# Softmax attention's keys normalised and rotated in the linear attention's last slots and passed on through DRAM

## The chip, the cores and the metric

The kernel runs on one core of a Trainium2 chip. The core has a matrix engine (TensorE, PE in the profile; its weight loads are a row of their own, PEld), a vector engine (VectorE, DVE), a scalar engine (ScalarE, ACT), a general engine (GpSimd, POOL, unused here) and a sync engine (SyncE, SP) whose queue issues nearly all DMA transfers. The engines run side by side, each through its own queue in order, and wait for each other on semaphores. SBUF is the on-chip memory of 128 partitions, PSUM the accumulators that PE writes, DRAM the memory outside. The metric is the time of one execution on the device in microseconds (us); lower is better.

## The reference

One encoder block over 1024 tokens of width 1024: two branches read the same normalised input, their gated sum goes through an output projection, and a feed-forward part follows. Cut to what matters here:

```python
h = _rms_norm(x, norm_mix_g[l])
proj = h @ w_in[l]          # q,k,v,r and gate codes of the linear attention; q,k,v of the softmax attention; gates
y_gla = _gla_branch(...) @ w_o_gla[l]
y_swa = _swa_branch(s_q, s_k, s_v, ...) @ w_o_swa[l]
merged = jax.nn.sigmoid(gate_a) * y_gla + jax.nn.sigmoid(gate_b) * y_swa
x = x + merged @ w_out[l]
x = x + (silu(gate) * up) @ w_ffn_out[l]      # with rms norm and w_ffn_in before
```

In the softmax attention branch the keys (2 heads of 128) and queries (8 heads of 128) are normalised per token and head, multiplied by a gain, and rotated; then each block of 128 tokens attends to itself and its two neighbours:

```python
q = _rope(_rms_norm(q.reshape(bsz, s, SWA_HEADS, hd), q_g), pos)
k = _rope(_rms_norm(k.reshape(bsz, s, hkv, hd), k_g), pos)
# _rope: concatenate([x1 * cos - x2 * sin, x2 * cos + x1 * sin])
```

The change moves the second of these two lines.

## The kernel before, in words

All products keep float32 accuracy: an operand is split into a high part (ACT copies it, rounded) and a low part (DVE subtracts), and three matmuls are added (`mm3`, L78). Weights stream from DRAM through `wunit` (L66): a load on SP, the high part on ACT, the low part on DVE.

The program runs through these stages, in order of time: input, statistics and the first projections (to about 250 us); the linear attention (to about 522 us); the softmax attention (to about 748 us); the gates and the output projection; the feed-forward part. The five remaining token-wise projections and eight feature-wise ones are not a stage of their own. They are generators of single matmuls in the list `dense` (L669), and both attentions are cut into slots: `slot` (L206) calls the parts of a slot and puts a given number of these matmuls between them (`fill`, L193), so that PE has work while the other engines prepare the next part. `need` (L202) runs `dense` on until a result has been stored.

PE's order is the order of the code, since both loops stand in `tc.manual_schedule` for that engine. The order of ACT, DVE and SP is made by a scheduler at build time: an earlier line goes first among what is ready, and what is not ready lets later lines pass. Once built, each queue runs in that order. Memory comes from pools of named tiles; a tag with `bufs=2` has two buffers, and a third tile of that tag waits for the first. A pool opened on the memory of closed pools waits until these are free as a whole.

- The first stage's pools are closed at L470 (`g0s.close()`). The linear attention's constants go into the pool `gc` (L472): `lrS` and `upS` (the gate codes and the gate weights, split), `mask`, and `tri`, loaded at L479. `upr` (L483) and `lrf` (L493) are the loads from which `upS` (L484, L485) and `lrS` (L495 to L498) are made.
- The linear attention's working tiles are in `gt` (L502, helper `gtile`, L509). It has 4 heads of 8 chunks, 46 slots (0 to 45). `at[t, j]` names the part `j` of slot `t`: `g_gates` (0), `g_powers` (6), `g_scores` (1), `g_out` (2), `g_back_out` (3), `g_turn` (4 or 5). The order within a slot is the tuple at L689. From slot 36 on only `g_back_out` and `g_turn` are left, and a slot has 12 dense matmuls, 18 in the last two. `g_turn` stores the output with `o<-ot` (L667).
- `proj_t("skv", 2)` is the third generator of `dense`. For each block `t` of 128 tokens it stores 512 values a token, two keys and two values, into the DRAM tile `scr["skv", t]` (L187).
- `glas.close()` (L690) frees the linear attention's pools. The softmax attention's constants are loaded from L707 on: `cosb`, `sinb`, `band`, `qg`, `kg`, `sink`.
- Its slots (`todo`, L894 on) hold, for key block `t`: `k_load` (L762) loads the block of keys and values into one tile `kvr` with one buffer; `k_prep` (L772) splits the values (`vSh`, `vSl`) and calls `norm_rope` (L735) for the keys; `k_turn` (L779) transposes the keys on PE into `kTh` and `kTl`. For queries: `a_load`, `a_prep`, `a_turn`, `a_scores` (maxima on DVE at L823, exponentials on ACT at L838), `a_probs` (transposed probabilities, copied at L858 and L859), `a_out`.
- `rsqrt` (L95) is Ln and Exp on ACT and four small DVE instructions that refine the result.

Of the kernel before, what the change touches and what calls it, by code (L numbers as in the profile page):

```python
# [8 lines left out]
F32 = mybir.dt.float32  # L9
FR = mybir.dt.float32r  # L10
U32 = mybir.dt.uint32
AF = mybir.ActivationFunctionType
ALU = mybir.AluOpType

P = 128
T = 1024
KT = 8
HT = 512
NH = 4
NC = 8  # L20
EPS = 1e-6
# [9 lines left out]
def body(tc, i, out):  # L31
    nc = tc.nc
    with ExitStack() as root:
# [8 lines left out]
        def nm(s):  # L42
            uid[0] += 1
            return f"{s}_{uid[0]}"
# [4 lines left out]
        def chtile(shape, dt=F32):  # L49
            return psc.tile(list(shape), dt, tag="ch", name=nm("ch"))  # L50
# [4 lines left out]
        def scratch(name, shape=(P, 512)):  # L55
            return dram.tile(list(shape), F32, tag=name, name=name)
# [4 lines left out]
        def load_const(pool, name, src, shape, dt=F32):  # L61
            t = pool.tile(list(shape), dt, tag=name, name=name)
            nc.sync.dma_start(out=t, in_=src)
            return t
# [23 lines left out]
        epst = cst.tile([P, 1], F32, tag="eps", name="eps")  # L88
# [6 lines left out]
        def rsqrt(dst, v, scale, epsv, eps_t, pool, shape, tag, tags=None):  # L95
            tags = tags or (tag + "l", tag + "t")
            l = pool.tile(list(shape), F32, tag=tags[0], name=nm("rl"))
            nc.scalar.activation(l, v, AF.Ln, bias=eps_t[:, 0:1], scale=scale)
            nc.scalar.activation(l, l, AF.Exp, scale=-0.5)
            t = pool.tile(list(shape), F32, tag=tags[1], name=nm("rt"))  # L100
            nc.vector.tensor_scalar(t, v, scale, epsv, op0=ALU.mult, op1=ALU.add)
            nc.vector.tensor_tensor(t, t, l, op=ALU.mult)
            nc.vector.scalar_tensor_tensor(t, t, -0.5, l, op0=ALU.mult, op1=ALU.mult)
            nc.vector.scalar_tensor_tensor(dst, t, 1.5, l, op0=ALU.add, op1=ALU.mult)
# [10 lines left out]
        scr = {}  # L115
# [77 lines left out]
        def fill(n):  # L193

            while n > 0 and dense:
                try:
                    next(dense[0])
                    n -= 1
                except StopIteration:
                    dense.pop(0)  # L200

        def need(key):  # L202
            while key not in scr:
                fill(12)

        def slot(stages, n):  # L206

            stages = [f for f in stages if f] or [lambda: None]
            done = 0
            for j, f in enumerate(stages):  # L210
                f()
                t = n * (j + 1) // len(stages)
                fill(t - done)
                done = t
# [195 lines left out]
        with tc.manual_schedule(engines={mybir.EngineType.PE}):  # L410
# [8 lines left out]
            for k in range(KT):  # L419
# [5 lines left out]
                c = slice((k % 4) * P, (k % 4 + 1) * P)  # L425
# [17 lines left out]
            for f in range(0, NG, 2):  # L443
                x_first(f)
                if f == 0:
                    for s in range(2):
                        v = chtile((P, HT))
# [22 lines left out]
        g0s.close()  # L470

        gc = glas.enter_context(tc.tile_pool(name="gc", bufs=1))  # L472
        lrS = gc.tile([98, T], FR, tag="lrS", name="lrS")
        upS = gc.tile([98, 2, 512], FR, tag="upS", name="upS")

# [13 lines left out]
        for s in range(2):  # L489
            c = slice(s * HT, (s + 1) * HT)  # L490
# [11 lines left out]
        gt = glas.enter_context(tc.tile_pool(name="gt", bufs=2))  # L502
# [6 lines left out]
        def gtile(tag, shape=(P, 256), dt=F32, bufs=2):  # L509
            return gt.tile(list(shape), dt, tag=tag, name=nm(tag), bufs=bufs)  # L510
# [148 lines left out]
        def g_turn(hd, c):  # L659
# [6 lines left out]
            for j in range(2):  # L666
# [2 lines left out]
        dense += [proj_t("v0", 0), proj_t("v1", 1), proj_t("skv", 2), proj_t("sq0", 3),  # L669
                  proj_t("sq1", 4)] + [proj_f(f"r{m}", 8 + m) for m in range(8)]  # L670

        at = {}
        last = 0
        for n in range(NH * NC):
            hd, c = divmod(n, NC)
            cb = hd * NC + NC + 4 + (NC - 1 - c)
            tt = cb + c % 2 + 2
            for j, (t, f) in enumerate(((n, g_gates), (n + 2, g_scores), (n + 4, g_out),
                                        (cb, g_back_out), (tt, g_turn))):
                if j or c % 2 == 0:  # L680
                    at[t, j + (j == 4 and c % 2)] = (f, hd, c)
                last = max(last, t)
            if c % 2 == 0:
                at[n + 1, 6] = (g_powers, hd, c)
        with tc.manual_schedule(engines={mybir.EngineType.PE}):
            fill(24)
            for t in range(last + 1):
                n = 46 if t < 2 else 30 if t < 4 else 15 if t < NH * NC + 4 else 12 if t < last - 1 else 18
                slot([(lambda v=at[t, j]: v[0](*v[1:])) if (t, j) in at else None for j in (0, 6, 5, 4, 3, 2, 1)], n)  # L689
        glas.close()  # L690


# [3 lines left out]
        sc_ = swas.enter_context(tc.tile_pool(name="swc", bufs=1))  # L696
        swe = swas.enter_context(tc.tile_pool(name="swe", bufs=2))
        stg = stgs.enter_context(tc.tile_pool(name="stg", bufs=4, side="right"))
        swl = stgs.enter_context(tc.tile_pool(name="swl", bufs=2, side="right"))
        swm = stgs.enter_context(tc.tile_pool(name="swm", bufs=1, side="right"))  # L700

        class sw:
            def tile(shape, dt, tag, name, bufs=2):
                pool = swm if tag in ("p", "ph", "pl") else swe if tag in (
                    "kvr", "sq2", "qn2", "sq4", "qn4", "qr", "qh", "ql") else swl
                return pool.tile(shape, dt, tag=tag, name=name, bufs=bufs)
        cosb = load_const(sc_, "cosb", i["c_cos"], (P, KT, 64))  # L707
        sinb = load_const(sc_, "sinb", i["c_sin"], (P, KT, 64))
        band = load_const(sc_, "band", i["c_band"], (P, 384))
        qg = load_const(sc_, "qg", i["qg"], (P, P))  # L710
        kg = load_const(sc_, "kg", i["kg"], (P, P))
        sink = load_const(sc_, "sink", i["sink"], (P, 8))
        kTh = sc_.tile([P, 2, T], FR, tag="kTh", name="kTh")
        kTl = sc_.tile([P, 2, T], FR, tag="kTl", name="kTl")
# [12 lines left out]
        def inv_norm(raw, n, sq, scale, epsv, eps_t):  # L727
            ss = sw.tile([P, n], F32, tag=f"ss{n}", name=nm("ss"))
            nc.scalar.activation(sq, raw[:, 0:n], AF.Square)
            nc.vector.tensor_reduce(ss, sq, axis=mybir.AxisListType.X, op=ALU.add)  # L730
            rs = sw.tile([P, n], F32, tag=f"rs{n}", name=nm("rs"), bufs=4)
            rsqrt(rs, ss, scale, epsv, eps_t, sw, (P, n), f"sn{n}")
            return rs

        def norm_rope(raw, n, t, gain, scale, epsv, eps_t):  # L735

            sq = sw.tile([P, n, P], F32, tag=f"sq{n}", name=nm("sq"))
            rs = inv_norm(raw, n, sq, scale, epsv, eps_t)
            qn = sw.tile([P, n, P], F32, tag=f"qn{n}", name=nm("qn"))
            for h in range(n):  # L740
                nc.vector.scalar_tensor_tensor(qn[:, h], raw[:, h], rs[:, h:h + 1], gain,
                                               op0=ALU.mult, op1=ALU.mult)
            c = cosb[:, t:t + 1].to_broadcast([P, n, 64])
            s = sinb[:, t:t + 1].to_broadcast([P, n, 64])
            b = sq
            nc.vector.tensor_tensor(b[:, :, 0:64], qn[:, :, 64:128], s, op=ALU.mult)
            nc.vector.tensor_tensor(b[:, :, 64:128], qn[:, :, 0:64], s, op=ALU.mult)
            nc.vector.tensor_tensor(qn[:, :, 0:64], qn[:, :, 0:64], c, op=ALU.mult)
            nc.vector.tensor_tensor(qn[:, :, 64:128], qn[:, :, 64:128], c, op=ALU.mult)
            nc.vector.tensor_tensor(qn[:, :, 0:64], qn[:, :, 0:64], b[:, :, 0:64], op=ALU.subtract)  # L750
            nc.vector.tensor_tensor(qn[:, :, 64:128], qn[:, :, 64:128], b[:, :, 64:128], op=ALU.add)
            return qn

        for h in range(8):
            for s in range(2):
                scr["b", h, s] = scratch(f"b{h}_{s}")
# [1 line left out]
        keys, att = {}, {}  # L758

        raws = {}  # L760

        def k_load(t):  # L762
            raws[t] = sw.tile([P, 4, P], F32, tag="kvr", name=nm("kvr"), bufs=1)
            need(("skv", t))
            nc.sync.dma_start(out=raws[t].rearrange("p a b -> p (a b)"), in_=scr["skv", t])

        def a_load(g, n):
            need((f"sq{g}", n))
# [1 line left out]
            nc.sync.dma_start(out=raws[g, n].rearrange("p a b -> p (a b)"), in_=scr[f"sq{g}", n])  # L770

        def k_prep(t):  # L772
            kv = raws.pop(t)
            v2 = kv[:, 2:4].rearrange("p a b -> p (a b)")
            nc.scalar.activation(vSh[t], v2, AF.Copy)
            nc.vector.tensor_tensor(vSl[t], v2, vSh[t].bitcast(F32), op=ALU.subtract)
            keys[t] = norm_rope(kv[:, 0:2], 2, t, kg, 1.0 / 128, EPS, epst)

        def k_turn(t):  # L779
            kt = chtile((P, 2, P))  # L780
# [114 lines left out]
        for n in range(2 * KT):  # L895
            g, t = divmod(n, KT)
# [5 lines left out]
            if n < KT:  # L902
                todo[n + 1].append((k_turn, n))
                todo[n].append((k_prep, n))
                if n:
                    todo[n - 1].append((k_load, n))
            todo[n].append((a_load, g, t))
        order = (a_probs, k_prep, a_prep, a_scores, a_turn, k_turn, a_out, k_load, a_load)
        k_load(0)
        with tc.manual_schedule(engines={mybir.EngineType.PE}):  # L910
            for t, v in enumerate(todo):
# [507 lines left out]
```

## Time and profile before

| what | value |
|---|---|
| median of 3 runs | 1643.52 us (1643.13 to 1643.59) |
| the profiled execution's own time | 1642.39 us, with a span of 1640.6 us |
| mean granted PE clock | 1.000 |
| DMA | 252.38 MB, mean 154 GB/s |
| raw keys and values stored (`skv<-st`) | 8, issued from 408.2 to 456.9 us |
| `kvr<-skv` loads in the attention | 8, issued from 526.6 to 593.9 us, 3.2 us to landing in the middle |
| DVE busy at 580 to 600, 600 to 620 us | 19.50 and 19.46 of 20 us |
| ACT busy at 330 to 400 us | 62.82 of 70 us |

How to read it: the span is from the first to the last instruction of the program. A row of the timeline gives start, duration, engine, line, operation, the tile written and the tiles read, shapes, a count where equal rows are merged, and in brackets how long the engine had been idle and what ended that. The matmuls overlap each other, so a duration of 0.39 us stands beside a start every 0.23 us. A row of waits reads "who waited <- for whom: us in total, times, longest". Starts count from the start of the span. "SPq" rows are DMA issues on SP's queue.

### The profile page before, as it was taken

How to read it: one execution, taken by the hardware profiler on the slowest of the kernel's cores; microseconds unless marked ns; L12 is line 12 of the kernel's file. 1: busy time of each engine (PE TensorE's matmuls, PEld its weight loads, DVE VectorE, ACT ScalarE, POOL GpSimd, SP SyncE). 2: the span in 40 equal slices, each digit the busy share in tenths (PEclk: the TensorE clock that was granted, in tenths of full speed). 3: DMA queues.
4: the chain of work that ended last, by engine and by line, in shares of the span. 5: the costliest groups of instructions: out<-in, count | busy, mean ns of one | idle time of the engine just before them, and what ended most of it. 6: DMA issues, size and time to landing. Idle time of an engine off the chain costs nothing.

```text
span 1640.6 us, 23222 instructions
## 1 busy us (share of the span) xinstructions
PE 1632.3 (99%) x7636; PEld 1357.1 (83%) x7636; DVE 1239.0 (76%) x2548; ACT 878.3 (54%) x1847; POOL 0.2 (0%) x4
## 2 busy tenths in 40 slices
PE   9999999999999999999999999999999999999999
PEld 7888888888888888887888888888888888888887
DVE  8766666788854998757885678877777788789655
ACT  8522234789986788775554557333333333354442
POOL 0000000000000000000000000000000000000000
PEclk9999999999999999999999999999999999999999
DMA  7444336444436533248765554443334443596433
GB/s 237 142 140 148 113 100 191 145 125 144 148 116 187 180 97 109 83 130 261 243 211 179 166 150 140 146 143 116 103 119 144 142 147 129 181 338 194 149 98 119
DMA packets 157497, 252.38 MB, mean 154 GB/s; under 512 B 18142, under 2 KB 43486, under 8 KB 157376
## 3 DMA queue, kind: packets, MB, share of 16 engines
q1 hardware_dynamic: 157376, 250.90, 48.5%
q8 instruction: 60, 0.98, 0.3%
q14 instruction: 61, 0.50, 0.1%
HBM read 183.46 MB, written 67.37 MB: 153 GB/s over the span
## 4 chain that ended last, share of the span: by engine, by line
PE 94%; DVE 2%; DMA 2%; ACT 1%; issue 0%; SPq 0%; ACTq 0%; DVEq 0%
PE mm L76 32%; PE mm L306 9%; PE mm L308 9%; PE mm L307 9%; PE ch L76 8%; PE mm L1232 7%; PE ch L1232 5%; PE ch L306 4%; PE ch L308 4%; PE ch L307 4%; PE ch L855 1%; DMA kvr<-skv 1%; DMA lo<-b 0%; PE ch L663 0%; PE ch L584 0%; PE ch L805 0%
## 5 line engine op out<-in xcount | busy, mean ns | idle before, releaser
L298 ACT ACTIVATE wh<-ws 128x512 fp32r<-128x512 f32 x132 | 83.3, 632 | 198.0 <-PE mm L307 103.9
L70 ACT ACTIVATE wh<-wr 128x512 fp32r<-128x512 f32 x226 | 140.7, 628 | 83.6 <-PE mm L76 59.7
L72 DVE TENSOR_TENSOR wl<-wr,wh 128x512 fp32r<-128x512 f32 x226 | 154.4, 687 | 36.5 <-ACT wh L70 35.9
L76 PE MATMUL mm<-wh,xh 128*128 128x512 f32 x320 | 132.3, 413 | 0.2 <-ACT st L186 0.2
L76 PE MATMUL mm<-wh,xl 128*128 128x512 f32 x320 | 130.6, 408 | 0.0
L76 PE MATMUL mm<-wl,xh 128*128 128x512 f32 x320 | 130.5, 408 | 0.0
L299 DVE TENSOR_TENSOR wl<-ws,wh 128x512 fp32r<-128x512 f32 x132 | 90.7, 687 | 29.6 <-ACT wh L298 28.4
L298 ACT ACTIVATE wh<-wr 128x512 fp32r<-128x512 f32 x69 | 43.6, 632 | 123.7 <-issue 49.6
L298 ACT ACTIVATE wh<-a 128x512 fp32r<-128x512 f32 x64 | 40.5, 633 | 90.3 <-PE ch L1232 42.3
L299 DVE TENSOR_TENSOR wl<-a,wh 128x512 fp32r<-128x512 f32 x64 | 44.2, 691 | 42.2 <-ACT wh L298 40.6
L76 PEld LDWEIGHTS mm<-wh,xh 128*128 128x128 f32 x320 | 60.4, 189 | 10.7 <-ACT st L186 0.6
L76 PEld LDWEIGHTS mm<-wl,xh 128*128 128x128 f32 x320 | 60.3, 189 | 10.3
L1232 PE MATMUL mm<-hh,wh 128*128 128x512 f32 x176 | 68.6, 390 | 0.0
L1232 PE MATMUL mm<-hh,wl 128*128 128x512 f32 x176 | 68.6, 389 | 0.0
L1232 PE MATMUL mm<-hl,wh 128*128 128x512 f32 x176 | 68.5, 389 | 0.0
L76 PEld LDWEIGHTS mm<-wh,xl 128*128 128x128 f32 x320 | 60.4, 189 | 9.8
L76 PE MATMUL mm<-xh,wh 128*128 128x512 f32 x160 | 65.6, 410 | 0.0
L76 PE MATMUL mm<-xl,wh 128*128 128x512 f32 x160 | 63.8, 399 | 0.0
L76 PE MATMUL mm<-xh,wl 128*128 128x512 f32 x160 | 56.5, 405 | 0.0
L1202 DVE TENSOR_TENSOR hl<-hr,hh 128x512 fp32r<-128x512 f32 x75 | 51.5, 686 | 4.5 <-ACT hh L1201 4.5
L1232 PE MATMUL ch<-hh,wl 128*128 128x512 f32 x132 | 51.4, 390 | 0.0
L1232 PE MATMUL ch<-hh,wh 128*128 128x512 f32 x132 | 51.4, 389 | 0.0
(566 smaller groups left out, 4877.3 us busy)
## 6 DMA issues: line engine op xcount, KB each, us to landing
wr<-in_w_fi_dram SPq DMA_DIRECT2D x102, 256.0 KB, 2.9
wr<-in_w_f_dram SPq DMA_DIRECT2D x80, 256.0 KB, 2.9
wr<-in_w_t_dram SPq DMA_DIRECT2D x80, 256.0 KB, 2.9
B<-c SPq DMA_DIRECT2D x44, 256.0 KB, 2.1
T<-tx SPq DMA_DIRECT2D x44, 256.0 KB, 2.7
a<-in_w_fo_dram SPq DMA_DIRECT2D x44, 256.0 KB, 5.2
hr<-T SPq DMA_DIRECT2D x44, 256.0 KB, 2.7
wr<-in_w_ob_dram SPq DMA_DIRECT2D x32, 256.0 KB, 3.1
```

The source lines that it names most:

```text
L70: nc.scalar.activation(h, raw, AF.Copy)
L72: nc.vector.tensor_tensor(l, raw, h.bitcast(F32), op=ALU.subtract)
L76: nc.tensor.matmul(o, a, b, start=start, stop=stop)
L298: nc.scalar.activation(h, src, AF.Copy)
L299: nc.vector.tensor_tensor(l, src, h.bitcast(F32), op=ALU.subtract)
L306: nc.tensor.matmul(o, h[:, c], x[kk][0], start=start and kk == 0, stop=False, skip_group_check=True)
L307: nc.tensor.matmul(o, h[:, c], x[kk][1], start=False, stop=False, skip_group_check=True)
L308: nc.tensor.matmul(o, l[:, c], x[kk][0], start=False, stop=kk == nk - 1, skip_group_check=True)
L855: nc.tensor.transpose(pt[:, h], a.p[:, h, (kb - a.b0) * P:(kb - a.b0 + 1) * P], ident)
L1202: nc.vector.tensor_tensor(l, r, h.bitcast(F32), op=ALU.subtract)
L1232: nc.tensor.matmul(ys[m], a[:, c], b, start=f0, stop=f1, skip_group_check=True)
```

## The change

Key blocks are no longer normalised and rotated by `k_prep` in the softmax attention, but by a new part `k_norm` of the linear attention, part 7 of slots 36 to 43, called last in its slot. It loads the keys' half of `scr["skv", t]`, computes the same as `norm_rope` did with `n = 2`, and stores the result into a new DRAM tile `scr["key", t]`. Its tiles come from the linear attention's pool `gt`, the rotation's scratch `sq2` with one buffer, `kvr` and `qn2` with two.

The cosine and sine tables and the keys' gain are loaded into `gc`, ahead of its other tiles; the attention still loads its own `cosb` and `sinb` for the queries, but no `kg`. `k_load` now makes two transfers, the values' half of `scr["skv", t]` into a `kvr` of half the size with two buffers instead of one, and the finished keys into a new tile `key` with two buffers. `k_prep` keeps the values' split alone. `norm_rope` is gone.

```diff
         gc = glas.enter_context(tc.tile_pool(name="gc", bufs=1))
+        cosk = load_const(gc, "cosk", i["c_cos"], (P, KT, 64))
+        sink_ = load_const(gc, "sink_", i["c_sin"], (P, KT, 64))
+        kg = load_const(gc, "kg", i["kg"], (P, P))
...
+        def k_norm(t):
+
+            need(("skv", t))
+            raw = gtile("kvr", (P, 2, P))
+            nc.sync.dma_start(out=raw.rearrange("p a b -> p (a b)"), in_=scr["skv", t][:, 0:256])
+            b = gtile("sq2", (P, 2, P), bufs=1)
+            ss = gtile("ss2", (P, 2))
+            nc.scalar.activation(b, raw, AF.Square)
+            nc.vector.tensor_reduce(ss, b, axis=mybir.AxisListType.X, op=ALU.add)
+            rs = gtile("rs2", (P, 2))
+            rsqrt(rs, ss, 1.0 / 128, EPS, epst, gt, (P, 2), "sn2")
+            qn = gtile("qn2", (P, 2, P))
+            for h in range(2):
+                nc.vector.scalar_tensor_tensor(qn[:, h], raw[:, h], rs[:, h:h + 1], kg, op0=ALU.mult, op1=ALU.mult)
...
+            scr["key", t] = scratch(f"key_{t}", (P, 256))
+            nc.sync.dma_start(out=scr["key", t], in_=qn.rearrange("p a b -> p (a b)"))
...
+        for t in range(KT):
+            at[NH * NC + 4 + t, 7] = (k_norm, t)
...
-                slot([(lambda v=at[t, j]: v[0](*v[1:])) if (t, j) in at else None for j in (0, 6, 5, 4, 3, 2, 1)], n)
+                slot([(lambda v=at[t, j]: v[0](*v[1:])) if (t, j) in at else None for j in (0, 6, 5, 4, 3, 2, 1, 7)], n)
...
-        kg = load_const(sc_, "kg", i["kg"], (P, P))
...
         def k_load(t):
-            raws[t] = sw.tile([P, 4, P], F32, tag="kvr", name=nm("kvr"), bufs=1)
+            raws[t] = sw.tile([P, 256], F32, tag="kvr", name=nm("kvr"))
             need(("skv", t))
-            nc.sync.dma_start(out=raws[t].rearrange("p a b -> p (a b)"), in_=scr["skv", t])
+            nc.sync.dma_start(out=raws[t], in_=scr["skv", t][:, 256:512])
+            keys[t] = sw.tile([P, 2, P], F32, tag="key", name=nm("key"))
+            nc.sync.dma_start(out=keys[t].rearrange("p a b -> p (a b)"), in_=scr["key", t])
...
         def k_prep(t):
-            kv = raws.pop(t)
-            v2 = kv[:, 2:4].rearrange("p a b -> p (a b)")
+            v2 = raws.pop(t)
             nc.scalar.activation(vSh[t], v2, AF.Copy)
             nc.vector.tensor_tensor(vSl[t], v2, vSh[t].bitcast(F32), op=ALU.subtract)
-            keys[t] = norm_rope(kv[:, 0:2], 2, t, kg, 1.0 / 128, EPS, epst)
```

The six rotation instructions left out of `k_norm` above are those of `norm_rope`, L746 to L751, with `cosk` and `sink_` for `cosb` and `sinb`.

More of the change, by code (lines that the diff above doesn't have):

```diff
@@ L670, in body @@
                   proj_t("sq1", 4)] + [proj_f(f"r{m}", 8 + m) for m in range(8)]
+        def k_norm(t):
[11 more added lines that the diff above has]
+                nc.vector.scalar_tensor_tensor(qn[:, h], raw[:, h], rs[:, h:h + 1], kg, op0=ALU.mult, op1=ALU.mult)
+            c = cosk[:, t:t + 1].to_broadcast([P, 2, 64])
+            s = sink_[:, t:t + 1].to_broadcast([P, 2, 64])
+            nc.vector.tensor_tensor(b[:, :, 0:64], qn[:, :, 64:128], s, op=ALU.mult)
+            nc.vector.tensor_tensor(b[:, :, 64:128], qn[:, :, 0:64], s, op=ALU.mult)
+            nc.vector.tensor_tensor(qn[:, :, 0:64], qn[:, :, 0:64], c, op=ALU.mult)
+            nc.vector.tensor_tensor(qn[:, :, 64:128], qn[:, :, 64:128], c, op=ALU.mult)
+            nc.vector.tensor_tensor(qn[:, :, 0:64], qn[:, :, 0:64], b[:, :, 0:64], op=ALU.subtract)
+            nc.vector.tensor_tensor(qn[:, :, 64:128], qn[:, :, 64:128], b[:, :, 64:128], op=ALU.add)
+            scr["key", t] = scratch(f"key_{t}", (P, 256))
+            nc.sync.dma_start(out=scr["key", t], in_=qn.rearrange("p a b -> p (a b)"))
         at = {}
@@ L704, in tile @@
                 pool = swm if tag in ("p", "ph", "pl") else swe if tag in (
-                    "kvr", "sq2", "qn2", "sq4", "qn4", "qr", "qh", "ql") else swl
+                    "kvr", "key", "sq4", "qn4", "qr", "qh", "ql") else swl
                 return pool.tile(shape, dt, tag=tag, name=name, bufs=bufs)
@@ L733, in inv_norm @@
             return rs
[L735 to L752, printed above, removed]
         for h in range(8):
```

## The prediction

> **What bounds the kernel now.** I read the page's head first, then the waits of the matmul engine, then its timeline around them.
>
> ```profile
> span 1640.6 us, 23222 instructions
> PE 1632.3 (99%) x7636; PEld 1357.1 (83%) x7636; DVE 1239.0 (76%) x2548; ACT 878.3 (54%) x1847; POOL 0.2 (0%) x4
> 250.27 5.44 PE mm L76 x24
> ```
>
> PE is busy through 99% of the span, and the chain of waits shows its pace: 24 matmuls in 5.44 us, 0.227 us each. The change adds and removes no PE instruction. So it can win only where PE stands still, and lose only where it makes PE stand still. The waits of PE list seven stops over the whole span; the largest is the first row below, and it and a small one lie in the attention's first slots.
>
> ```profile
> PE ch L76 <- DVE pl L859: 1.5, 1, 1.5
> 541.86 0.40 PE L76 MATMUL mm<-wh,xl 128*128 128x512 f32 x1
> 542.42 0.50 PE L76 MATMUL mm<-wh,xh 128*128 128x512 f32 x1 [0.16 <-ACT st L186]
> 575.23 0.62 PE L76 MATMUL mm<-xh,wl 128*128 128x512 f32 x2
> 577.37 0.44 PE L76 MATMUL ch<-kTh,sqh 128*128 128x384 f32 x1 [1.51 <-DVE pl L859]
> ```
>
> From start to start, less the pace: 542.42 - 541.86 - 0.23 = 0.33 us, and 577.37 - 575.23 - 2 x 0.227 = 1.68 us. Together 2.0 us: that is all the change can win where it takes work away. How full the other engines are, by stretch:
>
> ```profile
> 400.00:460.00 60.00, 60.00 (x346) 51.80 (x345) 50.11 (x154) 55.24 (x162) 0.00 (x0) 1.00 0.45 135
> 480.00:500.00 20.00, 20.00 (x100) 16.62 (x99) 9.63 (x25) 15.61 (x45) 0.00 (x0) 1.00 0.49 154
> 530.00:545.00 15.00, 14.84 (x66) 11.93 (x66) 14.95 (x49) 10.10 (x25) 0.00 (x0) 1.00 0.75 231
> 560.00:580.00 20.00, 18.47 (x96) 15.39 (x95) 19.43 (x74) 18.06 (x50) 0.00 (x0) 1.00 0.49 147
> ```
>
> Columns: length, then busy time of PE, weight load, DVE, ACT, POOL. At 530 to 580 DVE is full (14.95 of 15, 19.43 of 20); at 480 to 500 it is half empty; at 400 to 460 ACT is the tight one, with 60 - 55.24 = 4.8 us free.
>
> **What the change moves, and what it weighs.** The rows of one key block (block 2) and of the load tile:
>
> ```profile
> 547.62 0.40 ACT L729 ACTIVATE sq<-kvr 128x256 f32<-128x256 f32 x1
> 548.48 0.42 DVE L730 TENSOR_REDUCE ss<-sq 128x2 f32<-128x256 f32 x1
> 548.93 0.30 ACT L98 ACTIVATE rl<-ss,eps 128x2 f32<-128x2 f32 x1
> 549.26 0.20 ACT L99 ACTIVATE rl<-rl 128x2 f32<-128x2 f32 x1
> 551.03 0.16 DVE L104 SCALAR_TENSOR_TENSOR rs<-rt,rl 128x2 f32<-128x2 f32 x1
> 551.25 0.62 DVE L741 SCALAR_TENSOR_TENSOR qn<-kvr,rs,kg 128x128 f32<-128x128 f32 x2
> 551.92 0.29 DVE L746 TENSOR_TENSOR sq<-qn,sinb 128x128 f32<-128x128 f32 x1
> 552.92 0.29 DVE L750 TENSOR_TENSOR qn<-qn,sq 128x128 f32<-128x128 f32 x1
>   DMA kvr<-skv: 6.2, 6
> ```
>
> DVE per block: reduction 0.42, four small steps of 0.16, two gains 0.62, six rotation steps at 0.20 from start to start ((552.92 - 551.92) / 5), 1.2: about 2.8 us, 23 us for eight blocks. ACT: 0.40 + 0.30 + 0.20 = 0.9 us a block, 7 us in all. The last row: six times ACT stood still until a key-and-value load landed, 6.2 us together, about 1.0 each, because that tile had one buffer.
>
> *The attention's side.* 23 us of DVE leave a stretch where it is full, and value loads get two buffers. What held PE at 577.37:
>
> ```profile
> 571.00 0.60 PE L855 MATMUL ch<-ident,p 128*128 128x128 f32 x4
> 572.83 0.42 ACT L775 ACTIVATE vSh<-kvr 128x256 fp32r<-128x256 f32 x1 [0.23 <-DMA kvr<-skv]
> 573.15 0.70 ACT L838 ACTIVATE p<-p,nm,rs 128x384 f32<-128x384 f32 x1
> 576.02 1.05 ACT L858 ACTIVATE ph<-ch 128x512 fp32r<-128x512 f32 x2
> ```
>
> The transposed probabilities were in PSUM from 571.0 + 0.6 = 571.6, but ACT copied them at 576.02, behind a value split that waited on its load and the exponentials, whose maxima DVE had made late. Both causes are eased by the change. Bounds: 0 (the order on ACT stays as it is) to -2.0 us (both stops go). I take -1.7, near the full end, since the larger stop has two eased causes. The eight new key loads I cost at nothing: they can be asked for a slot ahead, as two buffers each allow; without that cover one costs PE at most what a value load now costs ACT, 1.0 us.
>
> *The linear attention's side.* `k_norm` stands in slots 36 to 43 of the linear attention, but only PE's order is by hand. Other engines take work as soon as its inputs and buffers allow:
>
> ```profile
> L187 SPq DMA_DIRECT2D skv<-st x8: 319/320/413, 408.2 to 456.9; - x8
> L1019 SPq DMA_DIRECT2D lx<-in_xT_dram x16: 327/328/423, 765.0 to 999.4; - x16
> L1021 DVE TENSOR_TENSOR lx<-mm,lx x16: 685/692/692, 881.5 to 1007.5; 128x512 f32<-128x512 f32 x16
>   ACT sg L981: 13.8, 10
> ```
>
> On SP a block now needs a load, a store and a second load for the one load before: at the 0.32 us of issue in the first row, 16 more issues, 5 us spread over a queue that is not full. The output projection's first input is asked for at 765.0 and used at 881.5, 116 us early. So I expect the first `k_norm` loads soon after 408.2, where the raw keys are stored, and some five blocks inside 400 to 460, where ACT is 92% busy. Such early work also blocks its queue: in the gating, ten early sigmoids held ACT 13.8 us, 1.4 each, for a load. Behind a waiting `Square` on ACT stand the copies that free PSUM for the linear attention, and PE waits for those; behind a store of a key that waits for DVE stand the weight loads on SP. Bounds: 0 (blocks wait for the half-empty stretch, where 0.9 us a block fits into 20 - 15.61 us) to 5 x (0.9 + 1.0) - 4.8 = +4.7 us (ACT overflows and PE pays all). I take +1.3, between them but nearer the low end, because PE has no stop at all there today.
>
> *The tables.* Three loads are put at the head of the linear attention's preparation, on the in-order SP queue.
>
> ```profile
> 239.96 0.46 SPq L483 DMA_DIRECT2D upr<-in_up_dram  x1
> 523.81 0.33 SPq L63 DMA_DIRECT2D cosb<-in_c_cos_dram  x1
> 525.13 0.43 SPq L63 DMA_DIRECT2D qg<-in_qg_dram  x1
> 244.07 1.06 ACT L484 ACTIVATE upS<-upr 98x1024 fp32r<-98x1024 f32 x1 [1.52 <-DMA lrf<-lr]
> 245.59 1.22 DVE L485 TENSOR_TENSOR upS<-upr,upS 34x1024 fp32r<-34x1024 f32 x1
> 253.88 1.22 DVE L498 TENSOR_TENSOR lrS<-lrf,lrS 32x1024 fp32r<-32x1024 f32 x1 [0.26 <-ACT lrS L497]
> 255.55 0.40 PE L76 MATMUL ch<-lrS,upS 98*128 98x256 f32 x2
> 526.00:528.00 2.00, 2.00 (x10) 1.66 (x9) 0.69 (x1) 0.63 (x1) 0.00 (x0) 1.00 0.99 323
> ```
>
> Three such loads took SP 525.13 - 523.81 = 1.3 us later in the kernel, so `upr` is asked for 1.3 us later; ACT's split, idle for a landing until 244.07, starts at 245.4 and ends at 246.4; DVE's L485 moves from 245.59 to about 246.5, and the run of DVE work behind it by the same 0.9 us. `lrS` is then done at 253.88 + 1.22 + 0.9 = 256.0, and PE, which wants it at 255.55, stands for 0.5 us. Bounds: 0 (DVE puts other ready work first) to +1.3; I take +0.5.
>
> The Trainium skill speaks against this edit more strongly: by "DMA: Bandwidth & Descriptors", section "Queues, rings and completion order", each DMA engine takes the descriptors of a ring in order, so the bytes of the tables, and not only their issue, go ahead of `upr`. Their 256 + 256 + 64 = 576 KB at the 323 GB/s of the last row are 1.8 us, which would make PE's stop 0.9 us instead of 0.5 and the time 1644.0; no row here shows a load behind these tables at this place.
>
> *The handover.* The attention's first load waits until all pools of the linear attention are free, the new ones among them:
>
> ```profile
> 512.51 0.59 PE L76 MATMUL ch<-thb,q2b 128*128 128x256 f32 x2
> 521.09 0.79 SPq L667 DMA_DIRECT2D o<-ot  x2
> ```
>
> cosb, at 523.81, goes out when the last of these stores lands. The first row is the last backward output, in slot 43, the slot of key block 7. Made as late as that, its chain of 552.92 + 0.29 - 547.62 = 5.6 us would end near 518 without its load and store, and with two transfers at 523.81 - 521.09 = 2.7 us each near 523.5: just covered. I cost it at 0; uncovered, it holds back SP and the weight loads queued there.
>
> **Sum**, against the profiled execution's own 1642.39 us (its span and 1.8 us around it): 1642.39 - 1.7 + 1.3 + 0.5 = 1642.5. The runs' median, 1643.52, is 1.1 above that execution, so the forecast for the median is **1643.6**: no change.
>
> **Rivals.** *All gain, no loss*: both stops go, blocks fit into free time, the tables cost nothing: 1642.39 - 2.0 + 1.1 = 1641.5. For it: PE is busy for 60.00 of 60 us at 400 to 460 now; against: ACT has 8% to spare there. *ACT overflows at 400 to 460*, the one that ends slower: 1642.39 - 1.7 + 0.5 + 4.7 + 1.1 = 1647.0. It decides once early `k_norm` work with its waits exceeds ACT's free 4.8 us; for it the 1.4 us waits of the sigmoids, against it the buffering between ACT and PE. *The stop at 577 stays*, as it is ACT's order and not DVE's load: 1642.39 + 1.3 + 0.5 + 1.1 = 1645.3. *The handover is late*: `k_norm` isn't taken early, and block 7 holds SP for, say, 3 us; PE then stands between 0 and 3 us, by how far its weights are ahead, in the middle 1.5 us: 1642.5 + 1.5 + 1.1 = 1645.1. Against it, the early orders above.
>
> **Chances.** Forecast 35%, all gain 22%, ACT overflow 20%, the stop stays 15%, late handover 8%. A measurement of this kernel can tell about 0.2%, 3.3 us, from no change. Only a surplus over "all gain" (other stops going by chance) is faster by more: 4%. Most of the overflow case and a little of the last two is slower by more: 18%. Within: 78%. The range runs from just under "all gain" to just over the overflow, 1641.2 to 1647.4.
>
> **What would show it.** Right: the 1.5 us wait on `pl` gone; DVE at 530 to 580 well below full; `k_norm`'s first `Square` before 430; a stop of PE near 255.6 at the first matmul on `lrS`; waits of ACT on the new `kvr` loads of about 1 us each. Wrong: PE stops of several us between 410 and 520, a first attention load later than 523.81, or a stop at 577 of the old size.

## The result, and the profile after

The change makes the kernel slower: 1656.62 us (median of 6 runs, 1654.67 to 1658.94) against 1643.55 us (6 runs of before, 1641.88 to 1644.17), ratio 1.0081 with a 95% interval of 1.0068 to 1.0094. The forecast was 1643.6, the range 1641.2 to 1647.4; the time lies 9 us outside it. The profiled execution of the changed kernel took 1654.67 us, 12.28 more than that of before.

The page's head, then the waits of PE (waited for, total us, times, longest us), of the changed kernel:

```profile
span 1652.9 us, 23277 instructions
PE 1634.2 (99%) x7636; PEld 1357.4 (82%) x7636; DVE 1241.2 (75%) x2548; ACT 878.6 (53%) x1847; POOL 0.2 (0%) x4
```

```profile
PE ch L76 <- DVE lrS L501: 11.5, 1, 11.5
...
PE ch L76 <- DVE mx L833: 0.6, 3, 0.2
```

The instructions of PE are as many as before, and the share that PE is busy still reads 99%. One row tells nearly all: PE stands once, for 11.5 us, at its first matmul on `lrS`. The wait of 1.5 us on `pl`, the largest of before, is gone. So the loss is not spread over the moved work; it sits where the linear attention starts, some 160 us ahead of the first key block. The timeline around that place, PE first:

```profile
255.16 0.39 PE L76 MATMUL mm<-wh,xl 128*128 128x512 f32 x1
267.06 0.80 PE L76 MATMUL ch<-lrS,upS 98*128 98x256 f32 x2 [11.51 <-DVE lrS L501]
267.65 0.63 PE L76 MATMUL mm<-wh,xh 128*128 128x512 f32 x1
...
270.64 0.44 PE L76 MATMUL mm<-wl,xh 128*128 128x512 f32 x1
```

Followed back, the chain is `lrS` from `lrf` and `upS` from `upr`, and so the two loads. The timeline of the SP queue (SPq rows are DMA issues) and of ACT in the changed kernel:

```profile
240.73 0.43 SPq L63 DMA_DIRECT2D tri<-in_c_tri_dram  x1
...
252.07 0.33 SPq L312 DMA_DIRECT2D k<-xc  x1
254.25 0.33 SPq L68 DMA_DIRECT2D wr<-in_w_t_dram  x1
254.93 0.38 SPq L486 DMA_DIRECT2D upr<-in_up_dram  x1
255.36 2.64 SPq L496 DMA_DIRECT2D lrf<-lr  x6
```

```profile
259.38 1.06 ACT L487 ACTIVATE upS<-upr 98x1024 fp32r<-98x1024 f32 x1 [3.17 <-DMA lrf<-lr]
264.70 1.06 ACT L500 ACTIVATE lrS<-lrf 96x1024 fp32r<-96x1024 f32 x1 [1.93 <-DVE lrf L499]
```

Before, `upr` went out at 239.96, right behind `tri`. Now `tri` goes out at 240.73, 1.2 us later than its 239.57 of before, close to the predicted 1.3 us of queueing, but `upr` follows only at 254.93: 15.0 us later than before, after the last store of the first stage (`k<-xc`, issued at 252.07) has landed. How long the transfers of this tile take, from the tile view of `k` at 244 to 260, and the row of the waits of SP (238 to 262) for `upr`:

```profile
DMA to landing us min/median/max: 2.4/2.6/2.8
```

```profile
SPq L486 <- DMA k<-xc: 0.2, 1, 0.2
```

That gives a landing at 254.5 to 254.9. A wait on that store, and not the queue, holds `upr` (weight loads `wr` went out between `tri` and `upr`); the rest (split, bias, `rstd`, split) runs behind it at its usual pace.

Where the 12.3 us between the two spans lie is read from three marks: the first matmul on `lrS` (255.55 before, 267.06 after), the first transpose of a key block, and the first matmul on `obh`, the end of the attention. The rows of the last two, of before (timeline; tile view: first and last start):

```profile
540.24 0.38 PE L782 MATMUL ch<-ident,qn 128*128 128x128 f32 x2
```

```profile
L76 PE MATMUL mm<-obh,wh x128: 388/390/495, 734.5 to 875.2; 128*128 128x512 f32 x128
```

and of the changed kernel:

```profile
554.91 0.38 PE L792 MATMUL ch<-ident,key 128*128 128x128 f32 x2
```

```profile
L76 PE MATMUL mm<-obh,wh x128: 388/390/399, 747.8 to 887.8; 128*128 128x512 f32 x128
```

| stretch of PE's fixed order, us | before | after | difference |
|---|---|---|---|
| start to first matmul on `lrS` | 255.55 | 267.06 | +11.5 |
| to first key transpose (linear attention) | 284.7 | 287.85 | +3.2 |
| to first matmul on `obh` (attention) | 194.3 | 192.9 | -1.4 |
| to the end of the span | 906.1 | 905.1 | -1.0 |
| span | 1640.6 | 1652.9 | +12.3 |

The last stretch has the same code in both kernels; its 1.0 us is what single executions differ by (with unchanged code there, three experiments gave 905.5 to 907.8).

Of the +3.2 us in the second stretch, a part is a consequence of the stop. Windows of the changed kernel (length, then busy time of PE, weight load, DVE, ACT, POOL, then PE's granted clock):

```profile
260.00:262.00 2.00, 0.00 (x0) 0.00 (x0) 1.50 (x2) 0.71 (x2) 0.00 (x0) 0.62 0.67 208
262.00:264.00 2.00, 0.00 (x0) 0.00 (x0) 1.97 (x5) 0.78 (x1) 0.00 (x0) 0.50 0.27 29
...
270.00:272.00 2.00, 2.00 (x8) 1.59 (x8) 1.95 (x6) 0.30 (x1) 0.00 (x0) 0.82 0.00 0
272.00:274.00 2.00, 2.00 (x11) 1.64 (x10) 1.26 (x4) 1.79 (x3) 0.00 (x0) 1.00 0.00 0
```

The granted clock falls to a half while PE stands and is full again only after 270. From 267.65 to 270.64 seven matmuls start, one every 0.43 us instead of 0.227, 1.4 us in all, and the two small ones at 267.06 take 0.59 to the next start instead of 0.24 (before's next row is at 255.79): together 1.8 us. The other 1.3 us are the moved work itself, as the experiments below show without the stop.

### The profile page after: what moved, and what is told of

Its sections match the earlier page's. It is cut to its first block, busy times and chain, and to the rows that moved or that the text cites. A ratio compares the mean times of both kernels' runs of the same rounds, so it can differ in the third digit from the quotient of the medians.

```text
span 1652.9 us, 23277 instructions
## 1 busy us (share of the span) xinstructions
PE 1634.2 (99%) x7636; PEld 1357.4 (82%) x7636; DVE 1241.2 (75%) x2548; ACT 878.6 (53%) x1847; POOL 0.2 (0%) x4
## 4 chain that ended last, share of the span: by engine, by line
PE 94%; ACT 2%; DVE 2%; DMA 1%; issue 1%; SPq 0%; DVEq 0%; ACTq 0%
PE mm L76 33%; PE mm L306 9%; PE mm L307 9%; PE mm L308 9%; PE ch L76 7%; PE mm L1242 7%; PE ch L1242 5%; PE ch L307 4%; PE ch L306 4%; PE ch L308 4%; PE ch L865 1%; PE ch L815 0%; PE ch L666 0%; PE ch L587 0%; DVE cs L547 0%
## 5 line engine op out<-in xcount | busy, mean ns | idle before, releaser
L1242 PE MATMUL ch<-hl,wh 128*128 128x512 f32 x132 | 51.4, 390 | 0.0
```

Source lines behind the costliest of these rows:

```text
L1242: nc.tensor.matmul(ys[m], a[:, c], b, start=f0, stop=f1, skip_group_check=True)
```

## The experiments

**Where the stop comes from.** The theory: memory. Of each partition the pool `gc` takes 4096 bytes for `lrS`, 4096 for `upS`, 2048 for `mask` and 512 for `tri`, 10752 together; the pool of `upr` and `lrf` (2 x 4096 = 8192) is opened right above it. Both lie where the first stage's pools lay: `ep` (12288 bytes), above it `xa` (8192), above it, from byte 20480, `x0`, whose tiles are stored up to the end of that stage. Before, the loads' pool ended at 10752 + 8192 = 18944, 1536 bytes short of `x0`. The tables and the gain add 2048 + 2048 + 512 = 4608 bytes, so it now ends at 23552, in `x0`. The rival is the one of the prediction: three more issues and their bytes ahead of `upr` on the queue.

*Tables elsewhere*: the change, but the three tiles in a pool of their own, opened after `gt`.

```diff
+        gk = glas.enter_context(tc.tile_pool(name="gk", bufs=1))
-        cosk = load_const(gc, "cosk", i["c_cos"], (P, KT, 64))
+        cosk = load_const(gk, "cosk", i["c_cos"], (P, KT, 64))
```

> The change with its three tables loaded into a pool of their own on top of the linear attention's working tiles, so that upr and lrf keep the place in memory they had before. Pool wait (upr and lrf wait for the first stage's pool x0, on whose memory the 4.5 KB of tables push them): upr is asked for at about 240 us again, the 11.5 us stop of PE at the first matmul on lrS and the half clock after it are gone, and the rest of the change shows alone: 1656.6 - 11.7 - 1.8 = 1643.1, between 1642 and 1644. Moved work (the key blocks in the linear attention cost PE): the stop goes but the time stays above 1646. Queue (the tables go ahead of upr): also about 1643, so this run does not tell it from the pool wait.

Measured: 1642.81 us against 1642.59, ratio 1.0003 (0.9994 to 1.0012). The stop is gone and with it the whole loss. The SP queue of this kernel, and PE's first matmul on `lrS`:

```profile
241.18 0.46 SPq L483 DMA_DIRECT2D upr<-in_up_dram  x1
...
251.62 0.86 SPq L63 DMA_DIRECT2D cosk<-in_c_cos_dram  x1
...
256.78 0.40 PE L76 MATMUL ch<-lrS,upS 98*128 98x256 f32 x2
```

`upr` is early again, and now the tables wait instead, where nobody needs them. But this moves both the memory and the place in the queue, so it doesn't decide between the two.

*Room alone*: the kernel before, with one tile in `gc` that nothing writes, of 1536 bytes and of 1600 bytes. No load is added.

```diff
         gc = glas.enter_context(tc.tile_pool(name="gc", bufs=1))
+        gc.tile([P, 384], F32, tag="room", name="room")
```

> The kernel before with 1536 bytes a partition of unused room ahead of the linear attention's constants; no table is loaded, no work moved. By the tile sizes upr and lrf then end exactly where pool x0 begins. Pool wait: no stop at lrS, 1643 to 1644 as before. Queue and moved work: 1643.5 as well, nothing they speak of is there.

> The same with 1600 bytes, so that the upper 64 bytes of upr's and lrf's pool lie on x0. Pool wait: upr is asked for only when the last store of the first stage has landed, near 254.5; PE stands about 11.5 us at the first matmul on lrS and runs at half clock for some 4 us after it; about 1643.5 + 13.4 = 1657, between 1655 and 1658. Queue and moved work: 1643.5, as nothing is loaded or moved.

Measured: 1641.79 us with 1536 bytes (0.9998, 0.9989 to 1.0007) and 1655.96 with 1600 (1.008, 1.0065 to 1.0096). The timeline with 1600 bytes:

```profile
251.99 0.33 SPq L312 DMA_DIRECT2D k<-xc  x1
...
254.90 0.38 SPq L484 DMA_DIRECT2D upr<-in_up_dram  x1
...
266.40 0.80 PE L76 MATMUL ch<-lrS,upS 98*128 98x256 f32 x2 [10.93 <-DVE lrS L499]
```

This settles it: with no load added, 64 bytes a partition, never written, decide 13 to 14 us, between the two sizes where the sum puts the edge. Of the 8192 bytes only 64 reach into `x0`, too few to touch both `upr` and `lrf`, and both go out late: the new pool waits as a whole. That it waits for the whole of the old pool, and not for the one tile under the 64 bytes, this run doesn't show: the last store reads a tile with the tag `xr00`, which is the first that `x0` was asked for and may lie just there.

*The neighbour moved*: the change as it is, but the first stage opens `w0` before `x0`, so that the loads' pool comes to lie on `w0`.

```diff
-        x0 = g0s.enter_context(tc.tile_pool(name="x0", bufs=1))
         w0 = g0s.enter_context(tc.tile_pool(name="w0", bufs=1))
+        x0 = g0s.enter_context(tc.tile_pool(name="x0", bufs=1))
```

> The change as it is, tables at the head, with the first stage's pools w0 and x0 in the other order, so that upr and lrf come to lie on w0, whose last reader ends near 238. Pool wait: no stop at lrS, 1642 to 1644. Queue: the tables are still loaded at the same place in the code, so most of the stop stays, above 1650. Moved work: above 1646.

Measured: 1643.3 us, ratio 1.0004 (0.9995 to 1.0012), no stop: PE is at `lrS` at 255.62. Here the tables are in `gc`, as in the change, and on the other neighbour the stop is gone. The order on the SP queue differs too:

```profile
237.94 0.39 SPq L486 DMA_DIRECT2D upr<-in_up_dram  x1
...
239.40 0.36 SPq L63 DMA_DIRECT2D cosk<-in_c_cos_dram  x1
```

`upr` goes out ahead of the tables, so this run alone doesn't tell the pool from the queue, and no run shows what all 576 KB of the tables ahead of `upr` would cost.

*The queue alone*: the kernel before with three small loads ahead of `tri` and `upr`, 768 bytes, so that the pool stays off `x0`.

```diff
+        for n, src in (("d0", "kg"), ("d1", "qg"), ("d2", "c_ident")):
+            load_const(gc, n, i[src][:, 0:64], (P, 64))
```

> The kernel of before with three more loads of 128x64 at the head of gc, issued on SP ahead of tri and upr; they add 768 bytes to each partition, less than the 1536 bytes that were spare, so the pool of upr and lrf stays off x0. This is the term that the prediction gave the tables, alone. If queueing is what the tables cost: upr is issued about 1.3 us later than 239.96, and TensorE stands 0.5 us (0 to 1.3) where it first needs lrS, time 1643 to 1644. If only the memory matters: upr is issued about 1.3 us later too, but no stop above 1 us is there and the first matmul on lrS starts between 255.5 and 256.5. A stop of 11 us would speak against both.

Measured: 1642.84 us, ratio 1.0004 (0.9995 to 1.0013). The rows:

```profile
239.94 0.33 SPq L63 DMA_DIRECT2D d<-in_kg_dram  x1
...
241.74 0.46 SPq L485 DMA_DIRECT2D upr<-in_up_dram  x1
...
256.44 0.50 PE L76 MATMUL ch<-lrS,upS 98*128 98x256 f32 x2 [0.37 <-DVE lrS L500]
```

`upr` is 1.8 us later than before, and PE stands for 0.4 us on `lrS`. That is the term that the prediction wrote down for the tables, 0.5, at its size: right as the price of three issues (these three move 96 KB, the tables 576), and not what the change had to pay.

**What the moved work costs in the linear attention.** Without the stop, the stretch from the first matmul on `lrS` to the first key transpose can be compared. It is the same within 0.2 us in all kernels with the code of before there (284.7 before, 284.7 with the room of 1536 bytes, 284.8 with the three loads) and 1.2 to 1.5 us longer with the key blocks (285.9 with the tables elsewhere, 286.2 with the neighbour moved, 286.0 in the kernel with one value buffer below). Why: ScalarE or VectorE? Windows of before, and of the change with its tables elsewhere:

```profile
420.00:460.00 40.00, 40.00 (x232) 34.56 (x231) 33.39 (x103) 35.94 (x106) 0.00 (x0) 1.00 0.45 133
```

```profile
420.00:460.00 40.00, 39.70 (x230) 33.87 (x229) 38.89 (x140) 36.91 (x113) 0.00 (x0) 1.00 0.46 145
```

The prediction looked at ACT, which gains 1.0 us here; DVE gains 5.5 and is full, 38.89 of 40. Four experiments start from the change with its tables elsewhere.

*Later blocks*: the raw block takes the tag of the linear attention's value tiles, so it can't be loaded early; its square gets two buffers.

```diff
-            raw = gtile("kvr", (P, 2, P))
+            raw = gtile("vr").rearrange("p (a b) -> p a b", a=2)
-            b = gtile("sq2", (P, 2, P), bufs=1)
+            b = gtile("sq2", (P, 2, P))
```

> The change with its tables in a pool of their own (as in e1_tables_above); the raw key block of k_norm shares the tag of the linear attention's value tiles (vr), so that a block can be loaded only when the value tile of its slot is free, and its square gets two buffers. Theory: the linear attention is longer by 1.24 us than before because the key blocks are taken up early, into the stretch in which ScalarE is full. Then the first Square moves from about 424 (in the time of e1) to after 450, the stretch from the first to the last matmul on lrS falls from 195.31 back to about 194.8 and the next one from 90.62 to about 89.9, and the whole takes about 1641.6 (1640.8 to 1642.6), ratio about 0.999. Rival: the blocks' own work costs this wherever it lies; then both stretches stay (195.3 and 90.6) and the time is that of e1, 1642.8, or blocks that come too late stop the first attention slots, 1643 to 1646.

Measured: 1643.48 us, 1.0002 (0.9993 to 1.0011). The first square moved from 422.9 to 465.7, and the stretch became longer, 286.6: to the last matmul on `lrS` it is back at 194.8 as expected, but after it a stop of 1.2 us stands at 498.06, on `ob` (`PE ch L667 <- ACT ob L661`). So the theory fails. The rival has the outcome right, that later blocks don't cost less, but not the places: the first stretch is shorter, and the cost comes behind it.

*Square on GpSimd*: takes the eight squares off ScalarE.

```diff
-            nc.scalar.activation(b, raw, AF.Square)
+            nc.gpsimd.tensor_tensor(b, raw, raw, op=ALU.mult)
```

> The change with its tables in a pool of their own (as in e1_tables_above), with the eight squares of k_norm on GpSimd, which does nothing in this stage, in place of ScalarE. In e1 the linear attention (first matmul on lrS to first key transpose) took 285.93 us against 284.69 before, with two stops of TensorE of 0.47 and 0.46 at 446.8 and 498.8. If ScalarE's share of the blocks (a square of 0.42 us each) causes that: the stops on ob go, the stretch is 284.7 to 285.2. If VectorE's share (eight operations, 2.4 us a block) causes it: both stops stay or grow, 285.9 to 286.8, time 1642.8 to 1643.7.

Measured: 1644.19 us, 1.0015 (1.0006 to 1.0024); stretch 286.8. The stop at 446.8 is gone, the one on `ob` has grown to 1.26 us, at 498.56. Taking the squares from ScalarE in this way doesn't help; but a square takes 0.61 us on GpSimd, against 0.42, and VectorE stands 1.8 us in all for three of them, so the run doesn't clear ScalarE.

*Products on GpSimd*: the four products of the rotation, off VectorE.

```diff
-            nc.vector.tensor_tensor(b[:, :, 0:64], qn[:, :, 64:128], s, op=ALU.mult)
+            nc.gpsimd.tensor_tensor(b[:, :, 0:64], qn[:, :, 64:128], s, op=ALU.mult)
```

> As e9, but it is the four products of the rotation in k_norm that go to GpSimd, from VectorE, and the square stays on ScalarE. VectorE then has some 1.1 us a block less to do, 9 us in all, in the stretch from 420 to 500, where it is 97% full in e1. If VectorE's fullness causes the 1.24 us: the stop at 446.8 goes and the stretch is 284.7 to 285.4, time about 1642. If ScalarE's does: the stops stay and the stretch is 285.9. If GpSimd slows VectorE down while both read their memory, VectorE's operations in 420 to 500 get longer than in e1 and the stretch is above 286.

Measured: 1652.18 us, 1.0061 (1.0049 to 1.0074): 10 us slower, the stretch is 295.2. The third expectation had the direction, but slower operations are the smaller part of the cause. Groups by line and shape of this kernel at 420 to 500 (count | busy us, mean ns | idle of the engine before them, and for whom), and the waits of its PE:

```profile
L697 DVE TENSOR_TENSOR qn<-qn,sq 128x128 f32<-128x128 f32 x6 | 2.9, 490 | 6.2 <-POOL qn L695 6.2
L696 DVE TENSOR_TENSOR qn<-qn,sq 128x128 f32<-128x128 f32 x6 | 1.7, 281 | 1.2 <-POOL qn L694 1.2
```

```profile
PE ch L667 <- ACT ob L661: 3.7, 4, 1.1
...
PE ch L76 <- ACT kb L620: 1.6, 1, 1.6
```

The two sums of the rotation stayed on VectorE and wait there for GpSimd, 7.4 us in total at the head of an in-order queue; behind them stand the operations that ScalarE and then PE wait for, which is argued from the order of the queue and not shown for each stop. This tells how dear a wait is in this queue, and nothing of the 1.2 us.

*No rotation*: the six operations are left out, and no wait is added.

> The change with its tables in a pool of their own (as in e1_tables_above), with the six operations of the rotation left out of k_norm, so that the attention's keys are normalised and not rotated. VectorE has 6 x 0.285 = 1.7 us a block less to do and no new wait is added. If VectorE's fullness from 420 to 460 is what the linear attention pays for: the stops at 446.8 and 498.8 go, the stretch from the first matmul on lrS to the first key transpose falls from 285.93 to about 284.7 (before), time about 1641.6. If it is ScalarE's part (load, square, the step of the root) or the order in which the blocks are taken: 285.7 to 286.8 and the stops stay.

Measured: 1641.84 us, 0.9994 (0.9984 to 1.0004); stretch 285.3 (PE's marks at 255.77 and 541.08), and both stops of PE at its transposes of `ob`, which the kernel with the tables elsewhere has (0.30 us each, at 446.76 and 498.78, ended by `ktl` of VectorE and `ob` of ScalarE), are gone. Half of the 1.2 us thus goes with the rotation's 1.7 us a block on VectorE, as one execution of each kernel has it. The remaining 0.6 us were not traced to one engine.

**The attention's side.** *One value buffer*: `kvr` of the attention with one buffer in place of two, tables elsewhere.

```diff
-            raws[t] = sw.tile([P, 256], F32, tag="kvr", name=nm("kvr"))
+            raws[t] = sw.tile([P, 256], F32, tag="kvr", name=nm("kvr"), bufs=1)
```

> The change with its tables in a pool of their own (as in e1_tables_above), but with one buffer for the attention's raw value rows (kvr) in place of two. Theory: the stop of TensorE that stood at 577 in before went because VectorE and ScalarE no longer normalise and rotate keys in the first slots; then it stays away and the stretch from the first key transpose to the first matmul on obh stays near 193.0, time 1642.8. Rival: it went because the next value rows can be loaded while the last are still in use; then the stop comes back, the stretch is near 194.2 and the time about 1644.

Measured: 1643.27 us, 0.9999 (0.999 to 1.0008). No wait on `pl` is listed, though ACT waits longer for the value loads than with two buffers. Waits of ACT with one buffer, and with two:

```profile
ACT vSh L787 <- DMA kvr<-skv: 6.6, 6, 2.4
```

```profile
ACT vSh L787 <- DMA kvr<-skv: 4.4, 6, 1.8
```

So it is not the second buffer that took the stop away; what is left is the keys' work, which left VectorE and ScalarE both, and no run tells the two apart. Its stretch came out at 193.6, between the two expectations: that length can't decide, since with before's code it was 194.3 in the profile of before, 193.1 with the room of 1536 bytes and 193.8 with the three loads. The wait on `pl` is the surer sign. It stands in every profile with the old attention (1.5 before, 0.8 with the room of 1536 bytes) and in none with the new. In its place the new one has short stops on `mx`, 0.6 us in three, against 0.2 in one.

```profile
PE ch L76 <- DVE pl L860: 0.8, 1, 0.8
```

The row is that of the kernel before with the room of 1536 bytes.

No version beats the kernel before by what can be measured, not even the one without the rotation, which leaves out work. Those with the tables elsewhere or the neighbour moved, and the blocks as the change has them, take 13 us less than the change and the same as before.

## Why the prediction was wrong, step by step

**The tables: the step that failed.** It put the price of three loads "at the head of the linear attention's preparation" at +0.5, bounds 0 to +1.3, from the queue alone. Three issues cost what it says (0.4 us measured with three small loads in their place). What it left out is what the loads' tiles do to the memory: 4608 bytes moved the next pool onto a pool that was still being stored from. The section on the kernel names this wait of pools; the sum never asked on which pools `upr` and `lrf` would then lie. The tile sizes stood in the kernel, and 1536 spare bytes against 4608 added could have been worked out from them. In place of +0.5 the term measured +11.5, and +1.8 behind it for the halved clock. Bounds built on the queue could not contain it. The paragraph beside it, by "DMA: Bandwidth & Descriptors", section "Queues, rings and completion order" of the Trainium skill, gave 0.9 us from the tables' bytes; no run tests it, since in the change `upr` waited for a store, and with the neighbour moved it went out ahead of the tables.

**The attention's side: right in mechanism, too large.** The wait on `pl` is gone, as predicted, and VectorE is relieved. The stretch 560 to 580 of before lies 15 us later in the changed kernel:

```profile
575.00:595.00 20.00, 20.00 (x104) 17.20 (x103) 16.96 (x58) 18.36 (x48) 0.00 (x0) 1.00 0.49 144
```

DVE is at 16.96 of 20, where it was at 19.43, while PE gets through 20.00 instead of 18.47. Predicted -1.7; between the two profiles it is -1.4. But before's own 1.5 us on `pl` was a large specimen: the same code gave 0.8 in other executions. Averaged over all profiles (four with the old attention, 193.5; eight with the new, 193.1) the stretch gains about 0.4 us, less than the 1.2 us by which executions with the old attention differ among themselves (193.1 to 194.3). A stop read from one execution was taken as a fixed gain.

**The linear attention's side: right in size, half right in cause.** +1.3 predicted, +1.2 to +1.5 measured. That the size is so near is partly luck, as the 1.3 was picked between bounds of 0 and 4.7. The blocks are taken early, as predicted: with the tables elsewhere the first `Square` is at 422.9, and in the changed kernel, which runs 11.5 us late by then, at 435.1.

```profile
L682 ACT ACTIVATE sq<-kvr x8: 403/420/482, 435.1 to 509.6; 128x256 f32<-128x256 f32 x8
```

But it put the loss on ACT, and half of it goes with VectorE's rotation, which the bounds didn't mention. What ACT's share is stays open.

**The handover: right, 0.** The rows of the changed kernel:

```profile
535.73 0.81 SPq L670 DMA_DIRECT2D o<-ot  x2
...
538.98 0.33 SPq L63 DMA_DIRECT2D cosb<-in_c_cos_dram  x1
```

From the last row of `ot` stores to the first load of the attention it is 3.3 us instead of 2.7, and no stop of PE follows it. The load is later than 523.81, which the prediction named as a sign that it is wrong; but what delays it is the shift of all that runs ahead of it.

**The value loads: right.** ACT waits for five of them, 6.1 / 5 = 1.2 us each, where about 1 was predicted:

```profile
ACT vSh L786 <- DMA kvr<-skv: 6.1, 5, 1.8
```

**The sum and the rivals.** Without the one failed term, -0.4 + 1.2 + 0 gives a kernel about 1 us slower: "no change", which the change with its tables elsewhere shows (1.0003). All five futures of the prediction took the pools' places as given, so none had a stop of 11 us: it was no question of how the chances were spread. "ACT overflows", the only rival on the slow side by much, did not occur.

## What to carry to other kernels

A new tile in a long-lived pool is first a shift of every pool above it: before costing its load, add up the sizes, see on which old pools the next ones come to lie, and when the last transfer of each of those lands. Here 1536 bytes more were free and 1600 cost 13 us, and opening the tables' pool after the urgent one takes all of it back. And a small stop seen in one execution is worth an average over several before it is booked as a gain.

## What the runs showed of the hardware

The clock of PE fell during the stop. In the changed kernel the last matmul ended at 255.16 + 0.39 = 255.55; if the 0.62 of the window 260 to 262 is one step from 1.00 to 0.50, it came at 260.5, 4.9 us later, and by the 0.82 of the window 270 to 272 it was back at 270.7, 3.7 us after PE resumed. The kernel with the room of 1600 bytes has a stop of nearly the same length, 10.9 us, and other times:

```profile
256.00:258.00 2.00, 0.00 (x0) 0.00 (x0) 0.69 (x1) 0.14 (x1) 0.00 (x0) 0.90 0.97 311
...
270.00:272.00 2.00, 2.00 (x8) 1.58 (x7) 1.29 (x6) 0.88 (x2) 0.00 (x0) 0.69 0.00 0
```

Its last matmul ended at 255.47. By the same reckoning its clock fell at 257.6, 2.1 us later, and was back at 271.2, 4.8 us after PE resumed at 266.40. The longer half clock cost more: its stretch from `lrS` to the first key transpose, with the code of before, is 287.2 instead of 284.7. So a stop of about 11 us cost 1.8 us more than itself in one execution and 2.5 in the other. The Trainium skill, "TensorE: Matmul & The Clock Gate", section "Part 1: The HAM clock gate (the "warmup" mystery)", states two clocks, full and half, a fall seen 5.2 us after the last matmul of one run, and a return after about 3.4 us of sustained work. The two clocks are seen here as well. The 4.9 and 3.7 us of the changed kernel come near its times, the 2.1 and 4.8 us of the other do not: when the clock steps differs between executions.

GpSimd slowed VectorE down. In the kernel with the products on GpSimd, its 128x128 product takes 0.46 us against 0.28 on VectorE, and VectorE's sum takes 0.53 when it starts beside a product and 0.28 when it doesn't:

```profile
472.95 0.53 DVE L697 TENSOR_TENSOR qn<-qn,sq 128x128 f32<-128x128 f32 x1 [1.48 <-POOL qn L695]
...
493.77 0.28 DVE L697 TENSOR_TENSOR qn<-qn,sq 128x128 f32<-128x128 f32 x1
```

```profile
472.87 0.46 POOL L694 TENSOR_TENSOR qn<-qn,cosk 128x128 f32<-128x128 f32 x1
...
493.00 0.46 POOL L694 TENSOR_TENSOR qn<-qn,cosk 128x128 f32<-128x128 f32 x1
```

The first sum overlaps the product that began 0.08 us ahead of it; the second starts 0.31 us after the last product has ended. The Trainium skill, "SBUF — State Buffer", section "SBUF: two separate sides", says that the two engines share a pair of ports by a lock that the first to start holds for its whole instruction, and that a VectorE operation with two inputs in SBUF takes part in it when the GpSimd one reads SBUF. The trace agrees as to a delay. That the sum is shut out for all of the product isn't shown: the product had 0.38 us left when the sum started, so a sum that only began its 0.28 us then would take 0.66, and it took 0.53.
